# Another queue for the loads of a bias slab, another engine for three constant fills, in a one-core decoder layer

## The chip, the cores and the metric

The kernel runs on one core of a Trainium2 chip. The metric is the device time of one execution in microseconds (us); the time of the kernel before is the median of 3 runs. A profile of one execution comes with it; its times count from the start of its span. Engines go by the profile's names: PE (TensorE, matmuls), PEld (its weight loads), DVE (VectorE), ACT (ScalarE), POOL (GpSimd), SP (SyncE). ACTq, SPq and POOLq are DMA issues that stand in the instruction list of ACT, SP or POOL.

## The reference, cut to what matters

One layer on a batch of 1, 256 tokens, width 2048, in float32. Three sub-layers follow each other; each ends in a layer norm:

```python
mix = hybrid_mixer(h, ...)                       # S5 | stick-breaking | NSA, one projection in, one out
h = layer_norm(ALPHA * h + mix, ...)
h = layer_norm(ALPHA * h + memory_cross_attention(h, mem, ...), ...)
h = layer_norm(ALPHA * h + conv_ffn(h, ...), ...)
```

In the mixer the columns of one input projection go to an S5 state-space group (a scan over time, a GELU and a gate `z * sigmoid(z @ w_glu + b)`), to 8 stick-breaking attention heads, and to 16 NSA heads. Each NSA head has three branches (compressed, selected and window keys), and the same relative-position bias, looked up by the distance `t - s`, is added to the logits of all three:

```python
s_s = jnp.einsum('bqgrd,bgqmd->bgrqm', qb, ks) * scale + bias_s
p_s = masked_softmax(s_s, dist_s >= 0)
```

## The kernel before, in words

**Matmuls.** Every weight matrix is streamed from HBM in chunks of 128 x 1024 floats (512 KB) by `weights` (L266): SP loads a chunk into one of 4 buffers `raw`, ACT rounds it into one of 3 buffers `hi` (L291), DVE subtracts to get the rest, `lo` (L292, 3 buffers), and PE multiplies three times for each pair of tiles, hi with hi, hi with lo, lo with hi (`mm3`, L306 to L308: 24 matmuls for a chunk). The result stands in one of 3 PSUM tiles `pj`.

**Order of the work.** A scheduler puts the instructions of each engine in a fixed list before the run, by priority lanes and by a timeline of its own; on the chip each engine works through its list in that order and waits in place for what an instruction needs.

**The stretch in question** lies in `mixer` (L509) and runs from about 200 to 385 us. `s5_out` (L755) computes two NSA key projections (`nsa_keys`, L941: ACT casts them into `kh` at L938, DVE makes the rest `kl` at L939), closes the S5 scan (its last output is `s5u`), takes its GELU on ACT (L765) after which a table of functions is loaded (L253), and multiplies by `w_glu`: four tiles `pj`, each of 12 matmuls, each evicted by ACT (L782) and worked on by DVE (an addition L784, two reciprocals L786, a product L787). Then `nsa_queries` (L964) projects the 16 heads' queries (8 pairs of chunks) into `nq` (ACT L970, DVE L971), and `nsa` (L974) runs the attention: for each head a pair of matmuls for each of two query tiles into a PSUM tile `mx` (L1011, L1012; 2 buffers), then DVE adds the bias from `slab` and takes row minima (L1015, L1017), copies the compressed scores into `tcs` (L1023), ACT takes exponentials, and so on. Projection matmuls that need no attention result stand between those of the attention.

**The bias slab.** `nsa_bias` (L839) computes the bias of each head by distance and writes 16 shifted copies of it to DRAM (`g_dr`). `nsa_slab` (L951) loads `slab`, 128 rows x 16 heads x 256 floats (2 MB), in 8 loads, each of 16 rows x 16 heads x 1 KB, so that row p holds the bias shifted by p. The tile takes the memory of `Es` (L639), the sines of the S5 part, which PE reads last in the S5 output matmuls (L685, in the trace L190). All three `V.memset` of the change stand at the head of `nsa`: `pc` (128 x 1024 floats, zero; written later by L1087, read by PE at L1059) and the first halves of two tiles `tcs` (128 x 60 floats).

Of the kernel before, what the change touches and what calls it, by code (L numbers as in the profile page):

```python
# [25 lines left out]
BIG = 1e30  # L26
# [138 lines left out]
class Parts:  # L165
# [9 lines left out]
    def range(self, k, n):  # L175
        if k == 0 and self.first is not None:
            assert n == 1
            return self.first
        return self.tiles[k // self.n][:, k % self.n:k % self.n + n]
# [18 lines left out]
class Program:  # L198
# [310 lines left out]
    def mixer(self):  # L509
# [6 lines left out]
        with ExitStack() as nsa:  # L516
            self.nsq = pool(nsa, "nsq", 1)
            self.slabp = pool(nsa, "slabp", 1)
            with ExitStack() as s5:
                self.s5p = pool(s5, "s5p", 1, "right")  # L520
                self.s5w = pool(s5, "s5w", 2, "right")
                self.s5_tables()
                self.load_x()
                with ExitStack() as st:
                    self.sbp = pool(st, "sbp", 1)
                    self.sbw = pool(st, "sbw", 2)
                    self.stick_breaking()
                self.nsk = pool(nsa, "nsk", 1)
                self.nsa_compress()
                self.nsa_values()  # L530
                self.s5_out()
            self.resp = pool(self.ctx, "resp", 1, "right")
            self.R = self.resp.tile([128, 2, D], F32, name="R")
            self.mixq = pool(self.ctx, "mixq", 1, "right")
            self.mix += [self.mixq.tile([128, 4, 2, 256], F32R, name=f"mix{i}")
                         for i in range(2, 4)]
            with ExitStack() as st:
                self.nsp = pool(st, "nsp", 1, "right")
                self.nsw = pool(st, "nsw", 2, "right")
                self.nsa_slab()  # L540
                self.nsa_queries()
                self.nsa()
# [408 lines left out]
    def nsa_slab(self):  # L951


        g_dr, n = self.g_dr, 128 // SKEW

        self.nq = self.nsp.tile([128, 8, 2, 256], F32R, name="nq")
        self.slab = self.slabp.tile([128, NH, 256], F32, name="slab", tag="Es")
        with self.lane("first"):
            for c in range(n):
                src = bass.AP(g_dr.tensor, g_dr.offset + 127 - c,  # L960
                              [[384 - n, SKEW], [SKEW * 384, NH], [1, 256]])
                self.nc.scalar.dma_start(self.slab[c:128:n], src)

    def nsa_queries(self):  # L964
        a, V, S, q = self.a, self.nc.vector, self.nc.scalar, self.nq
# [8 lines left out]
    def nsa(self):  # L974
        nc, a, V, S = self.nc, self.a, self.nc.vector, self.nc.scalar
# [8 lines left out]
        def qcol(h):  # L984
            return 4 * (h // 8) + 2 * (h // 4 % 2) + h % 2


        pc = p.tile([128, 2, NH, 32], F32, name="pc")
        V.memset(pc, 0.0)
        tcs = [p.tile([128, 2, 4, NC_], F32, name=f"tcs{i}") for i in range(2)]  # L990
        for t in tcs:
            V.memset(t[:, 0], BIG)
        halves = lambda t: t.rearrange("p (c k) -> p c k", c=2)
        for quad in range(4):
            o = self.pq.tile([128, 2, 256], F32, name="pa")
            start = [None, None]
            for b in range(2):
                n = 128 if b else 128 + NK
                for gl in range(2):
# [3 lines left out]
                    for r in range(2):  # L1003
                        h = h0 + r
                        kh, kl = (k[:, h // 8, gl].rearrange("p c n -> p (c n)") for k in ks[b])
                        t = qcol(h)
# [329 lines left out]
```

## Time and profile before

| | |
|---|---|
| median of 3 runs | 1294.0 us (1293.86 to 1295.22) |
| the profiled execution's own time | 1293.79 us |
| its span in the trace | 1292.0 us |
| mean granted TensorE clock | 0.992 of full speed |
| busy, share of the span | PE 97%, PEld 90%, DVE 68%, ACT 51%, POOL 1% |
| moved by DMA | 237.37 MB, mean 184 GB/s |

The own time is what the runs are timed by; the span is what the trace shows of it, and 1.8 us lie around it. Busy shares are means over stages with different limits. A group of instructions with the same line and form is shown with its count; "idle before <-X" names what ended the idle time of the engine just before.

### The profile page before, as it was taken

Reading aid. Unit: us, or ns where it says so; the run is one execution under the profiler, and the core shown is the slowest. Engines: PE = TensorE matmul, PEld = TensorE weight load, DVE = VectorE, ACT = ScalarE, POOL = GpSimd, SP = SyncE. Lnnn points to the kernel's source line nnn. Section 1 sums busy time; section 2 is a strip of 40 time slices with the busy share of each in tenths; the row PEclk is TensorE's granted clock in tenths of the full one; section 3 lists DMA queues with packets and bytes.
Section 4 is the critical chain, followed back from the end, with each engine's and each line's share of the span. In section 5 each row is a group of like instructions: output and inputs, shape, how many; then the busy total and the mean of one; then the engine's idle time right before and its main releaser. Section 6 shows DMA issues by size and latency. Waiting matters only on the chain.

```text
span 1292.0 us, 23010 instructions
## 1 busy us (share of the span) xinstructions
PE 1254.6 (97%) x9222; PEld 1160.8 (90%) x9222; DVE 883.8 (68%) x1510; ACT 659.9 (51%) x1032; POOL 13.3 (1%) x23
## 2 busy tenths in 40 slices
PE   7999999999999999899999999999999999999996
PEld 7788898988779899799999999999999988888896
DVE  7799896877765675776666666666666654544557
ACT  6884434666554355455555555555555543334342
POOL 0200000000000000000000000000000000000000
PEclk9999999999999999999999999999999999999998
DMA  8653348633447564445555565565655755656573
GB/s 306 192 167 128 99 137 224 186 117 103 131 168 279 189 208 151 137 142 194 192 192 195 196 195 191 191 193 194 196 196 190 254 193 195 195 184 199 187 228 130
DMA packets 68886, 237.37 MB, mean 184 GB/s; under 512 B 7787, under 2 KB 10652, under 8 KB 68012
## 3 DMA queue, kind: packets, MB, share of 16 engines
q1 hardware_dynamic: 64720, 230.21, 53.7%
q10 hardware_dynamic: 3276, 3.47, 1.2%
q0 software_dynamic: 784, 2.23, 0.9%
q8 instruction: 72, 1.18, 0.4%
q14 instruction: 34, 0.28, 0.1%
HBM read 231.82 MB, written 2.49 MB: 181 GB/s over the span
## 4 chain that ended last, share of the span: by engine, by line
PE 76%; DVE 3%; ACT 1%; issue 1%; DMA 0%; DVEq 0%; ACTq 0%
PE pj L306 14%; PE pj L307 14%; PE pj L308 14%; PE pj L314 9%; PE pj L316 9%; PE pj L315 9%; PE pa L1048 2%; DVE lo L292 1%; PE mx L1011 1%; PE mx L1012 1%; DVE R L1144 1%; DVE R L1149 1%; PE op L1041 0%; PE pb L1041 0%; ACT hi L291 0%
## 5 line engine op out<-in xcount | busy, mean ns | idle before, releaser
L292 DVE TENSOR_TENSOR lo<-raw,hi 128x1024 fp32r<-128x1024 f32 (+2 forms) x403 | 488.5, 1212 | 339.0 <-ACT hi L291 337.9
L291 ACT CAST hi<-raw 128x1024 fp32r<-128x1024 f32 (+2 forms) x403 | 419.8, 1042 | 510.7 <-PE pj L307 276.4
L307 PE MATMUL pj<-mix,hi 128*128 128x256 f32 x1380 | 381.9, 277 | 0.0
L306 PE MATMUL pj<-mix,hi 128*128 128x256 f32 x1380 | 381.1, 277 | 0.0
L308 PE MATMUL pj<-mix,lo 128*128 128x256 f32 x1380 | 381.0, 276 | 0.0
L307 PEld LDWEIGHTS pj<-mix,hi 128*128 128x128 f32 x1380 | 259.2, 188 | 0.1
L308 PEld LDWEIGHTS pj<-mix,lo 128*128 128x128 f32 x1380 | 259.2, 188 | 0.1
L306 PEld LDWEIGHTS pj<-mix,hi 128*128 128x128 f32 x1380 | 259.1, 188 | 0.2
L306 PE MATMUL pj<-A,hi 128*128 128x256 f32 x496 | 141.2, 288 | 8.6 <-ACT hi L291 8.6
L308 PE MATMUL pj<-A,lo 128*128 128x256 f32 x496 | 139.2, 288 | 4.2 <-DVE lo L292 4.0
L307 PE MATMUL pj<-A,hi 128*128 128x256 f32 x496 | 140.4, 286 | 0.0
L306 PEld LDWEIGHTS pj<-A,hi 128*128 128x128 f32 x496 | 95.9, 194 | 11.2 <-ACT hi L291 9.3
L308 PEld LDWEIGHTS pj<-A,lo 128*128 128x128 f32 x496 | 94.6, 194 | 8.1 <-DVE lo L292 5.6
L307 PEld LDWEIGHTS pj<-A,hi 128*128 128x128 f32 x496 | 96.1, 194 | 1.9 <-issue 1.9
L315 PE MATMUL pj<-lo,act 128*128 128x512 f32 (+1 forms) x280 | 96.8, 347 | 0.0
L316 PE MATMUL pj<-hi,act 128*128 128x512 f32 (+1 forms) x280 | 96.8, 347 | 0.0
L315 PE MATMUL pj<-lo,A 128*128 128x512 f32 (+2 forms) x288 | 96.3, 336 | 0.0
L316 PE MATMUL pj<-hi,A 128*128 128x512 f32 (+2 forms) x288 | 95.6, 333 | 0.0
L314 PE MATMUL pj<-hi,A 128*128 128x512 f32 (+2 forms) x288 | 91.0, 334 | 0.0
L314 PE MATMUL pj<-hi,act 128*128 128x512 f32 (+1 forms) x280 | 89.7, 347 | 0.0
L315 PEld LDWEIGHTS pj<-lo,A 128*128 128x128 f32 x288 | 54.1, 188 | 6.5 <-issue 1.1
L315 PEld LDWEIGHTS pj<-lo,act 128*128 128x128 f32 x280 | 52.9, 189 | 6.6
(324 smaller groups left out, 1809.5 us busy)
## 6 DMA issues: line engine op xcount, KB each, us to landing
raw<-in_w_up SPq DMA_DIRECT2D x176, 512.0 KB, 4.2
raw<-in_w_down SPq DMA_DIRECT2D x92, 512.0 KB, 3.3
raw<-in_win_c SPq DMA_DIRECT2D x48, 512.0 KB, 3.9
raw<-in_w_out SPq DMA_DIRECT2D x32, 512.0 KB, 4.0
raw<-in_win_sv SPq DMA_DIRECT2D x8, 512.0 KB, 4.7
raw<-in_wk_m SPq DMA_DIRECT2D x8, 512.0 KB, 4.9
raw<-in_wv_m SPq DMA_DIRECT2D x8, 512.0 KB, 4.2
raw<-in_wq SPq DMA_DIRECT2D x8, 512.0 KB, 4.1
```

Of the source, the lines that this page charges most:

```text
L291: self.last_hi = nc.scalar.copy(hi[:, :n], raw[:, :n])
L292: self.last_lo = nc.vector.tensor_sub(lo[:, :n], raw[:, :n], hi[:, :n].bitcast(F32))
L306: mm(ps, hi, ah, start=start, stop=False)
L307: mm(ps, hi, al, start=False, stop=False)
L308: self.last_mm = mm(ps, lo, ah, start=False, stop=stop)
L314: mm(ps, ah, hi, start=start, stop=False)
L315: mm(ps, ah, lo, start=False, stop=False)
L316: self.last_mm = mm(ps, al, hi, start=False, stop=stop)
L1011: mm(zs, q[:, t, gl, qs], kh[:, 0:m], start=True, stop=False)
L1012: mm(zs, q[:, t, gl, qs], kl[:, 0:m], start=False, stop=True)
L1048: ins = mm(o[64 * r:64 * r + 64, gl, 128 * c:256], vv[:, c, v, :], pt[:, k0:k1], start=start[r] is None, stop=False, skip_group_check=True)
L1144: ins = V.scalar_tensor_tensor(r, r, mean, self.gb[:, 0, c0:c1], ALU.subtract, ALU.mult)
```

## The change

The 8 loads of `slab` are issued by POOL and no longer by ACT, and the three constant fills at the head of `nsa` run on POOL and no longer on DVE. Sizes, addresses and results are the same.

```diff
@@ nsa_slab
             for c in range(n):
                 src = bass.AP(g_dr.tensor, g_dr.offset + 127 - c,
                               [[384 - n, SKEW], [SKEW * 384, NH], [1, 256]])
-                self.nc.scalar.dma_start(self.slab[c:128:n], src)
+                self.nc.gpsimd.dma_start(self.slab[c:128:n], src)
@@ nsa
         pc = p.tile([128, 2, NH, 32], F32, name="pc")
-        V.memset(pc, 0.0)
+        nc.gpsimd.memset(pc, 0.0)
         tcs = [p.tile([128, 2, 4, NC_], F32, name=f"tcs{i}") for i in range(2)]
         for t in tcs:
-            V.memset(t[:, 0], BIG)
+            nc.gpsimd.memset(t[:, 0], BIG)
```

The scheduler then writes other lists for PE, DVE and ACT from here to the end of the mixer. SP's list is the same, and PE's is the same up to the second attention head. Three places follow, rows of the lists as they stand, without the number at their start; tiles that share a buffer pool are told apart by numbers.

ACT's list where S5 ends, one piece of the difference (- before, + changed). `kh_2091` is the first key tile, `s5u<-s5u` the GELU:

```order
 L938 CAST kh_2091<-pj 64x2x128 x2
-L962 DMA slab<-g_dr 16x16x256 x8
-L291 CAST hi<-raw 128x1024 x2
-L938 CAST kh_2091<-pj 64x2x128 x2
 L765 ACTIVATE s5u<-s5u 128x1024
 L253 ACT_TABLE_LOAD
 L979 ACTIVATE gate<-gate 128x96
 L291 CAST hi<-raw 128x1024
```

The eight loads leave ACT's list, and the GELU with its table load now stands ahead of the two weight casts and the key casts that were behind the loads. On POOL the eight loads stand right behind its last instruction so far, the memset of `kl_2544`, and behind them the fills of `pc` and of the two `tcs`, which are the last work of POOL in the program.

DVE's list at the gate of the S5 part, before and changed. `s5z_2705` and `s5z_2726` are the gate tiles of the first two `w_glu` results, and `kl1_2544<-pj_2613` frees the PSUM tile that the first query projection, `pj_2803`, takes:

```order
L784 TENSOR_SCALAR s5z_2705<-s5z_2705 128x256
L786 RECIPROCAL s5z_2705<-s5z_2705 128x128 x2
L939 TENSOR_TENSOR kl1_2544<-pj_2613,kh1_2543 64x256
L292 TENSOR_TENSOR lo_2837<-raw_2834,hi_2836 128x1024
L787 TENSOR_TENSOR s5z_2705<-s5z_2705,s5u_198 128x256
L784 TENSOR_SCALAR s5z_2726<-s5z_2726 128x256
```

```order
L784 TENSOR_SCALAR s5z_2705<-s5z_2705 128x256
L786 RECIPROCAL s5z_2705<-s5z_2705 128x128 x2
L292 TENSOR_TENSOR lo_2837<-raw_2834,hi_2836 128x1024
L784 TENSOR_SCALAR s5z_2726<-s5z_2726 128x256
L939 TENSOR_TENSOR kl1_2544<-pj_2613,kh1_2543 64x256
L787 TENSOR_TENSOR s5z_2705<-s5z_2705,s5u_198 128x256
```

The subtraction that frees the PSUM tile now stands behind a weight chunk's `lo` and behind the addition of the second gate tile.

PE's list at the first attention heads, before and changed. `mx_3348` is the tile of the second head and `mx_3385` that of the third; `pj_2998` is the fourth query projection:

```order
L1011 MATMUL mx_3348<-kh0_2091,nq_2793 128x272
L1012 MATMUL mx_3348<-kl0_2092,nq_2793 128x272
L1011 MATMUL mx_3385<-kh0_2091,nq_2793 128x256
L1012 MATMUL mx_3385<-kl0_2092,nq_2793 128x256
L1011 MATMUL mx_3385<-kh0_2091,nq_2793 128x272
```

```order
L1011 MATMUL mx_3348<-kh0_2091,nq_2793 128x272
L1012 MATMUL mx_3348<-kl0_2092,nq_2793 128x272
L306 MATMUL pj_2998<-A_92,hi_3001 128x256
L307 MATMUL pj_2998<-A_92,hi_3001 128x256
L308 MATMUL pj_2998<-A_92,lo_3002 128x256
```

Before, the third head follows the second at once; now a whole chunk, 24 projection matmuls, stands between them. From here to the end of the attention its matmuls are spread over more projection matmuls than before.

## Rows read from the trace of the kernel before

**Rows 1.** The page's busy time of each engine, with its share of the span and its instructions.

```profile
PE 1254.6 (97%) x9222; PEld 1160.8 (90%) x9222; DVE 883.8 (68%) x1510; ACT 659.9 (51%) x1032; POOL 13.3 (1%) x23
```

**Rows 2.** Busy time by stretch: the stretch, its length, busy us (and instructions begun) of PE, PEld, DVE, ACT and POOL, then the granted PE clock, the share of the 16 DMA engines and GB/s.

```profile
222.00:224.00 2.00, 0.45 (x4) 0.24 (x3) 0.00 (x0) 0.41 (x1) 0.00 (x0) 1.00 1.09 201
224.00:226.00 2.00, 0.56 (x3) 0.35 (x3) 1.33 (x2) 1.96 (x4) 0.00 (x0) 1.00 1.15 197
226.00:228.00 2.00, 2.00 (x10) 2.00 (x11) 1.45 (x2) 1.96 (x3) 0.00 (x0) 0.53 1.15 193
228.00:230.00 2.00, 2.00 (x13) 2.00 (x13) 0.90 (x3) 1.99 (x4) 0.00 (x0) 0.62 1.08 217
232.00:234.00 2.00, 1.49 (x14) 1.32 (x13) 1.93 (x3) 1.40 (x3) 0.00 (x0) 1.00 0.91 305
234.00:236.00 2.00, 1.23 (x11) 1.01 (x9) 1.49 (x2) 1.84 (x4) 0.00 (x0) 1.00 0.45 113
236.00:238.00 2.00, 0.76 (x6) 0.77 (x7) 1.90 (x5) 1.79 (x5) 0.00 (x0) 1.00 0.77 254
258.00:260.00 2.00, 1.50 (x13) 1.28 (x11) 1.97 (x8) 1.46 (x3) 0.00 (x0) 1.00 0.51 186
260.00:262.00 2.00, 0.00 (x0) 0.00 (x0) 1.97 (x9) 1.95 (x8) 0.00 (x0) 1.00 0.69 256
262.00:264.00 2.00, 1.52 (x11) 1.55 (x12) 1.84 (x8) 1.02 (x5) 0.00 (x0) 0.91 0.77 215
264.00:266.00 2.00, 2.00 (x12) 2.00 (x11) 1.96 (x10) 0.99 (x4) 0.00 (x0) 0.50 0.13 53
266.00:268.00 2.00, 2.00 (x15) 2.00 (x15) 0.43 (x4) 0.04 (x1) 0.00 (x0) 0.73 0.00 0
270.00:384.00 114.00, 114.00 (x742) 91.98 (x742) 81.41 (x302) 70.82 (x192) 0.00 (x0) 1.00 0.38 125
```

**Rows 3.** Who waited for whom, PE alone, from 195 to 260 us and then from 260 to 420 us: us in total, times, longest.

```profile
PE pj L306 <- ACT hi L291: 2.2, 1, 2.2
PE pj L306 <- ACT s5z L782: 2.0, 1, 2.0
PE pj L308 <- DVE lo L292: 0.8, 1, 0.8
PE pj L306 <- DVE kl L939: 0.5, 1, 0.5
...
PE mx L1011 <- DVE nq L971: 3.0, 1, 3.0
```

**Rows 4.** ACT's instructions in order of time: start, length, instruction, and the idle time before it.

```profile
214.40 9.10 ACTq L962 DMA_DIRECT2D slab<-g_dr  x8
223.59 1.99 ACT L291 CAST hi<-raw 128x1024 fp32r<-128x1024 f32 x2 [9.04 <-DMA slab<-g_dr]
226.38 1.06 ACT L765 ACTIVATE s5u<-s5u 128x1024 f32<-128x1024 f32 x1
227.45 1.28 ACT L253 ACT_TABLE_LOAD   x1
236.71 0.47 ACT L782 ACTIVATE s5z<-pj,s5nbg 128x256 f32<-128x256 f32 x1
250.29 1.06 ACT L291 CAST hi<-raw 128x1024 fp32r<-128x1024 f32 x1 [1.29 <-PE pj L307]
253.01 1.06 ACT L291 CAST hi<-raw 128x1024 fp32r<-128x1024 f32 x1 [1.25 <-PE pj L307]
```

**Rows 5.** The instructions that write or read `slab`: count, ns least/median/most, first and last start, forms; and the time from issue to landing of its loads.

```profile
L1015 DVE CUSTOM_DVE_ANT_0 tt<-mx,slab x32: 259/285/292, 259.3 to 361.1; 128x128 f32<-128x128 f32 x32
...
L962 ACTq DMA_DIRECT2D slab<-g_dr x8: 540/630/1221, 214.4 to 223.0; - x8
...
DMA to landing us min/median/max: 8.5/10.3/12.2
```

**Rows 6.** DVE's instructions in order of time, columns as in rows 4.

```profile
214.96 0.47 DVE L190 SCALAR_TENSOR_TENSOR s5u<-s5u,s5prm,pa 128x256 f32<-128x256 f32 x1
...
224.67 2.36 DVE L292 TENSOR_TENSOR lo<-raw,hi 128x1024 fp32r<-128x1024 f32 x2 [8.78 <-ACT hi L291]
...
237.24 0.28 DVE L784 TENSOR_SCALAR s5z<-s5z 128x256 f32<-128x256 f32 x1
237.55 1.76 DVE L786 RECIPROCAL s5z<-s5z 128x128 f32<-128x128 f32 x2
239.34 0.43 DVE L939 TENSOR_TENSOR kl<-pj,kh 64x256 fp32r<-64x256 f32 x1
...
256.03 0.91 DVE L989 MEMSET pc<- 128x1024 f32 x1 [0.16 <-DVE lo L292]
```

**Rows 7.** The loads that POOL issues early in the program, of the S5 inputs (128 KB each): count, ns least/median/most, first and last start; and from issue to landing.

```profile
L496 POOL DMA_DIRECT2D s5us<-Ec x12: 550/551/693, 35.4 to 42.5; - x12
...
DMA to landing us min/median/max: 3.3/5.3/8.8
```

**Rows 8.** Busy time by stretch, columns as in rows 2, for the gate of the S5 part and for the time of POOL's early loads.

```profile
235.00:258.00 23.00, 20.86 (x179) 20.45 (x179) 21.27 (x35) 13.37 (x24) 0.00 (x0) 1.00 0.52 170
34.00:44.00 10.00, 10.00 (x49) 8.33 (x48) 6.34 (x10) 8.73 (x17) 6.69 (x12) 1.00 0.88 224
```

**Rows 9.** POOL's last instruction, a fill of 128 x 1024 floats.

```profile
181.93 0.95 POOL L931 MEMSET kl<- 128x1024 f32 x1 [15.32 <-PE mx L877]
```

## The prediction

> **What bounds the kernel now.** I read the busy shares first [rows 1]. PE is busy 97% of the span, the other engines far less, so a change counts only where PE stands still or runs slowly near it. I therefore read the busy time by stretch around the loads of `slab` [rows 2]. From 270 to 384 us PE is busy 114.00 of 114 us at clock 1.00: work taken off DVE or ACT there buys nothing. The losses lie ahead of that, in 222 to 268 us. Next I asked who waited for whom [rows 3], and then read the waiting engines in order of time. ACT spends 9.10 us, from 214.40 on, on issuing the eight loads, and its next weight cast comes at 223.59 after 9.04 us [rows 4]. DVE, whose `lo` needs that cast, does nothing for 8.78 us up to 224.67 [rows 6]. PE uses up the chunks cast ahead and then stands.
>
> **PE's losses, as they are.** Each is the length of a stretch less its busy time, or the busy time times what the clock lacks to 1.00 [rows 2].
> 1. PE out of weights, 222 to 226 us: 1.55 + 1.44 = 3.0 us. By the waits, 2.2 for `hi` and 0.8 for `lo` [rows 3].
> 2. Just behind it the granted clock is 0.53 and 0.62, near the 1.2 GHz level, from 226 to 230: 0.94 + 0.76 = 1.7 us.
> 3. 232 to 238 us: 0.51 + 0.77 + 1.24 = 2.5 us; these are the waits for the key remainder (L939, 0.5) and for the eviction of the first gate tile (L782, 2.0).
> 4. 258 to 264 us: 0.50 + 2.00 + 0.48 = 3.0 us, the wait of an attention matmul for `nq` from L971. DVE is busy 1.97 us of each 2 there: it is still working off what the 8.78 us put back.
> 5. After that stop the clock is 0.50 and 0.73 from 264 to 268: 1.0 + 0.5, and 0.1 before it, is 1.6 us.
>
> Together 11.8 us.
>
> **The loads leave ACT.** `s5u` is written by 214.96 + 0.47 = 215.4 us [rows 6]. The GELU (1.06) and the table load (1.28) follow, then a small activation on 128 x 96, at most the 0.47 that the larger 128 x 256 takes, and the next weight cast, 1.06 [rows 4]. That cast ends by about 219.3, and its `lo`, 2.36/2 = 1.18 [rows 6], by about 220.5. PE ran dry only at about 222.4 [rows 2]. So losses 1 and 2 go whole; the cover is some 2 us.
>
> **The gate stretch.** The changed list of DVE puts `kl1_2544<-pj_2613` behind a `lo` and a second L784. The wait of loss 3 thereby moves: the second and third gate tiles need PSUM tiles long free, and the tile waited for is the one that the first query projection takes. DVE does, behind the eviction of the first gate tile (0.47 on ACT [rows 4]), 0.28 + 1.76 (L784 and the reciprocals) + 1.18 (`lo`) + 0.28 + 0.43 (L939) [rows 6]: 3.93 us, with the eviction 4.4, and with hand-over between engines, which I estimate at 0.1 to 0.6 in all, 4.5 to 5.0. Meanwhile PE has three gate tiles of 12 matmuls. A chunk's 24 matmuls set the 2.72 us from one cast to the next, 250.29 to 253.01 [rows 4], so 36 take 4.08. The new wait is 0.4 to 0.9; I take 0.9. The eviction of the second gate tile can stand behind a weight cast of 1.06 on ACT: between 0 and 1.06, I take 0.4, since PE has one more tile to work on. For the third head, 24 matmuls (2.72 us) now come ahead of the matmul that waited 3.0: I keep 0.2. New losses: 1.5 us, between 0 and 4.7, the upper end being one whole stop such as 4 with its slow clock, 3.0 + 1.7.
>
> **The loads on POOL.** POOL's last work is a fill at 181.93 [rows 9], so it waits for the same end of the S5 matmuls that ACT waited for and begins at about 214.3. Its earlier loads took 0.55 us each to issue [rows 7]: eight are 4.4 us on an engine with nothing queued but the fills. No row shows loads of this shape on POOL, so I bound their landing. Below: 214.3 + 4.4 + 5.3 (the median landing) = 224. Above: the twelve early loads, 1.5 MB in all, take from 35.4 to 42.5 + 8.8 = 51.3, which is 15.9 us [rows 7], scaled to 2 MB 21.2 us, so 235.5. I take 235, as those are the nearest rows. The first reader is L1015, at 259.3 before [rows 5]; with losses 1 to 3 gone (7.2) and the new 1.3 added it stands at about 253.4. That leaves 18 us of cover. If it were gone, each us late would be a us of PE.
>
> The same bytes share the DMA engines with the weight stream: 2 MB over some 18 us are 117 GB/s, and a chunk of 0.524 MB every 2.72 us is 193. The sum, 310, stands against 305 in the best stretch of two us [rows 2]. The chunks that lie ready in 3 `hi` and 4 `raw` buffers cover up to 19 us, so I put this at nothing; its price is in rival A.
>
> **The fills.** DVE loses a fill of 0.91 [rows 6] and two small ones. POOL does the large one in 0.95 [rows 9], at a time when it is otherwise idle, and the tiles are read only in the attention. DVE's gain lies in loss 4 and isn't counted again.
>
> **Sum.** 11.8 - 1.5 = 10.3 us. The profiled execution's own time is 1293.8, 0.2 below the median: 1293.8 - 10.3 = 1283.5 us.
>
> **Rivals.**
> A. *One stop stays.* Either DVE still is late with `nq`, or the weights come late while `slab` loads. For it: DVE is busy 21.27 of 23 us from 235 to 258 [rows 8], so it works off a debt slowly, and 310 GB/s is at the edge. Against: DVE starts 8.8 us earlier. One stop with its slow clock costs 4.7, the gain is 5.6 to 5.8 and the time 1288.
>
> B. *Hardly any gain.* The idle time is only displaced: the attention, whose lists are rewritten, gives it back. From 270 to 384 PE has no idle time that could hide an added wait, DVE is busy 81.41 and ACT 70.82 of 114 [rows 2], so there is room, which speaks against it. A gain of 10.3 less two stops of 4.7 would be 0.9: 1292.9.
> The Trainium skill, in "DMA: Bandwidth & Descriptors", section "Issuing engines are not separate DMA queues", says that issuing on several engines saves only the issuing sequencer's time, which is usually small beside the transfer. By that the change would bring almost nothing, about 1293 us. This trace differs on the size: 9.10 us on ACT against 8.5 to 12.2 from issue to landing [rows 4, 5].
>
> C. *Slower.* POOL could issue only while DVE stands still. From 235 to 258 DVE leaves 1.73 us of 23 [rows 8], a share of 0.075, so 4.4 us of issuing would need 58 us: the last load is issued at about 273, lands 8.8 later at 281.6, and L1015, due at 253.4, waits 28.2, with 1.7 for the clock behind it. Less the 10.3 gained that is 19.6 slower: 1313. It decides from a landing at about 262 on, 48 us after the start and over twice my upper bound. Against it: POOL's early issues kept to 550 to 693 ns while DVE was busy 6.34 of 10 us [rows 7, 8].
> The Trainium skill names such a mechanism in "SBUF — State Buffer", section "SBUF: two separate sides": a load issued from GpSimd has its descriptors written there, and this stops while VectorE runs an operation in a mode that takes both ports. By it the time would lie between 1283 and 1313, depending on how many of DVE's operations are of that kind, which no row here shows.
>
> **How the numbers follow.** The forecast as worked out has 0.62, A 0.23, B 0.06, C 0.04, and a gain above 12 us, which would need something outside the sum, 0.05. The forecast's own bounds are 1282.0 (no new loss) to 1285.2 (new losses of 3.2, between the 1.5 taken and the 4.7). For 8 in 10 the range reaches down to 1281.0, a little of the larger gain, and up over A to 1288.5; out of it fall B, C and the rest of the larger gain. A measurement of this kernel tells about 0.2% from no change, 2.6 us. Faster by more: the forecast, A and the larger gain, 0.90. Within: B and a part of C, 0.06. Slower: 0.04, the rest of C and mishaps of its size.
>
> **What would show it.** ACT has no 9 us gap at 214, and the GELU starts at about 215.4. PE is busy 2.00 of 2 us from 222 to 230 at clock 1.00. PE's largest wait in the gate is that of the first query projection for L939, below 1 us, and the wait of L1011 for L971 shrinks from 3.0 to a few tenths. L1015 first runs at about 253. POOL's eight issues take about 0.55 us each and the last load lands by 235. If PE's busy time grows by as much as its idle time falls, or the stretch after 264 has a slow clock again, the sum is wrong, and A or B holds; if L1015 waits for `slab`, C.

## The result, and the profile after

The changed kernel takes 1286.15 us (median of 4 runs, 1285.80 to 1287.67), the kernel before 1293.93 on the same chip: the ratio is 0.994, with a 95% interval from 0.9923 to 0.9957. The gain is 7.8 us. Forecast were 10.3 and 1283.5; the time lies in the range, between the forecast and rival A.

The page's first line, as [rows 1]:

```profile
PE 1251.7 (98%) x9222; PEld 1158.2 (90%) x9222; DVE 882.1 (69%) x1507; ACT 660.3 (51%) x1032; POOL 18.9 (1%) x34
```

Busy time by stretch in the changed kernel, columns as in [rows 2]:

```profile
222.00:224.00 2.00, 2.00 (x20) 2.00 (x19) 1.94 (x3) 1.95 (x5) 0.00 (x0) 1.00 1.00 201
224.00:226.00 2.00, 2.00 (x20) 2.00 (x19) 1.24 (x2) 0.17 (x1) 0.00 (x0) 1.00 1.07 213
226.00:228.00 2.00, 2.00 (x20) 2.00 (x19) 0.86 (x1) 1.79 (x3) 0.00 (x0) 1.00 1.04 240
228.00:230.00 2.00, 2.00 (x19) 2.00 (x18) 0.80 (x2) 0.00 (x0) 0.00 (x0) 1.00 1.00 252
230.00:232.00 2.00, 0.79 (x7) 0.58 (x5) 0.00 (x0) 0.59 (x1) 0.00 (x0) 1.00 1.05 283
232.00:234.00 2.00, 0.23 (x2) 0.23 (x2) 1.48 (x2) 1.66 (x4) 0.00 (x0) 1.00 1.04 293
234.00:236.00 2.00, 1.47 (x12) 1.26 (x11) 1.97 (x4) 0.85 (x1) 0.00 (x0) 1.00 0.96 313
236.00:238.00 2.00, 1.38 (x11) 1.38 (x12) 1.91 (x4) 1.30 (x4) 0.00 (x0) 1.00 0.42 162
...
260.00:262.00 2.00, 2.00 (x20) 2.00 (x19) 1.97 (x8) 0.99 (x4) 0.00 (x0) 1.00 0.26 102
...
264.00:266.00 2.00, 2.00 (x15) 1.49 (x15) 1.87 (x5) 2.00 (x8) 0.00 (x0) 1.00 0.23 92
```

From 222 to 230 us PE is now busy throughout at clock 1.00, and so it is from 258 to 270. What is left lies between 230 and 238 us: PE stands 1.21 + 1.77 + 0.53 + 0.62 = 4.1 us, in two pieces of 2.98 and 1.15 us, with no slow clock behind them. I call the two together the stop in the gate. The losses of 11.8 us have become 4.1, which is 7.7 us; the span fell by 8.4 (1292.0 to 1283.6) and the median by 7.8.

Who waited for whom in that stretch (answers to [rows 3]; us in total, times, longest):

```profile
ACT hi L291 <- DMA raw<-in_win_c: 5.0, 2, 3.5
...
PE pj L306 <- ACT s5z L782: 4.1, 2, 3.0
...
ACT hi L291 <- DMA raw<-in_w_glu: 1.9, 1, 1.9
```

ACT in order of time (answers to [rows 4]):

```profile
215.28 1.06 ACT L765 ACTIVATE s5u<-s5u 128x1024 f32<-128x1024 f32 x1 [0.91 <-DVE s5u L190]
216.35 1.28 ACT L253 ACT_TABLE_LOAD   x1
...
217.84 1.03 ACT L291 CAST hi<-raw 128x1024 fp32r<-128x1024 f32 x1
...
231.41 1.04 ACT L291 CAST hi<-raw 128x1024 fp32r<-128x1024 f32 x1 [3.53 <-DMA raw<-in_win_c]
...
233.25 0.47 ACT L782 ACTIVATE s5z<-pj,s5nbg 128x256 f32<-128x256 f32 x1
```

The waits name the eviction L782 as what PE stood for. The order in time shows what is behind it. PE had finished the tile by 230.8. Its eviction stands in ACT's list behind a weight cast, and that cast waited 3.53 us for its chunk to arrive. The second piece comes about in the same way: the next L782 stands behind the next cast, which waited 1.43 us for its chunk. The stop is a late weight load, seen through ACT's fixed list.

Where the chunk was: the DMA queues in three stretches of 2 us of the changed kernel, from 216, 224 and 232 us (q1 carries SP's weight loads, q0 POOL's `slab`; packets, MB, share of the 16 engines; below them the loads issued in the stretch, with the us from issue to landing):

```profile
q1 hardware_dynamic: 75, 0.29, 42.0%
q0 software_dynamic: 51, 0.17, 35.8%
slab<-g_dr POOLq DMA_DIRECT2D x5, 256.0 KB, 14.8
...
q0 software_dynamic: 128, 0.41, 103.5%
q1 hardware_dynamic: 2, 0.00, 1.2%
raw<-in_win_c SPq DMA_DIRECT2D x1, 512.0 KB, 12.5
...
q1 hardware_dynamic: 147, 0.54, 94.5%
q0 software_dynamic: 14, 0.05, 9.2%
raw<-in_win_c SPq DMA_DIRECT2D x1, 512.0 KB, 6.2
```

The eight loads are all issued within 4.49 us. From 220 to 226 they have the DMA engines nearly to themselves, though weight loads issued at 220.16 and 223.14 stand ready. The one of 220.16 lands 11.2 us after issue and one of 224.85 12.5, against 4.4 for a chunk issued at 210. SP's issues around it (start, length):

```profile
214.88 0.33 SPq L772 DMA_DIRECT2D raw<-in_w_glu  x1
...
220.16 0.33 SPq L270 DMA_DIRECT2D raw<-in_win_c  x1
...
223.14 0.33 SPq L270 DMA_DIRECT2D raw<-in_win_c  x1
```

Of POOL itself (answers to [rows 7, 9]):

```profile
214.47 4.49 POOL L962 DMA_DIRECT2D slab<-g_dr  x8 [31.77 <-DMA raw<-in_win_c]
250.97 0.96 POOL L989 MEMSET pc<- 128x1024 f32 x1 [32.02 <-DVE s5z L787]
```

### The profile page after: what moved, and what is told of

Same layout as the page of the kernel before. It is cut to its first block, busy times and chain, and to the rows that moved or that the text cites. A ratio compares the mean times of both kernels' runs of the same rounds, so it can differ in the third digit from the quotient of the medians.

```text
span 1283.6 us, 23034 instructions
## 1 busy us (share of the span) xinstructions
PE 1251.7 (98%) x9222; PEld 1158.2 (90%) x9222; DVE 882.1 (69%) x1507; ACT 660.3 (51%) x1032; POOL 18.9 (1%) x34
## 4 chain that ended last, share of the span: by engine, by line
PE 92%; DVE 3%; ACT 2%; DMA 2%; issue 1%; SPq 0%; ACTq 0%; DVEq 0%
PE pj L306 17%; PE pj L308 17%; PE pj L307 17%; PE pj L314 10%; PE pj L315 10%; PE pj L316 10%; PE pa L1048 2%; DMA raw<-in_win_c 1%; PE pa L190 1%; PE mx L877 1%; ACT hi L291 1%; PE mx L1011 1%; DVE lo L292 1%; PE mx L1012 1%; DVE R L1144 0%
## 5 line engine op out<-in xcount | busy, mean ns | idle before, releaser
L306 PEld LDWEIGHTS pj<-A,hi 128*128 128x128 f32 x496 | 94.5, 191 | 8.2 <-ACT hi L291 6.3
L307 PEld LDWEIGHTS pj<-A,hi 128*128 128x128 f32 x496 | 94.5, 191 | 1.6 <-issue 1.6
L316 PEld LDWEIGHTS pj<-hi,act 128*128 128x128 f32 x280 | 52.9, 189 | 6.6
```

The lines of the kernel that those rows point to most:

```text
L306: mm(ps, hi, ah, start=start, stop=False)
L307: mm(ps, hi, al, start=False, stop=False)
L316: self.last_mm = mm(ps, al, hi, start=False, stop=stop)
```

## The experiments

Two theories stood against each other. Traffic: the weights are late because 2 MB are queued ahead of them at once. Order: the stop comes from the new lists, with evictions behind casts on ACT and a longer chain on DVE. In e3_no_loads, e4_twice, f_sp, g_sp and e5_sp_at_once the lists of PE, DVE and ACT agree with the changed kernel's row for row; g_sp is f_sp once more and g_changed the changed kernel once more. The changed kernel's two ratios, 0.9940 and 0.9958, are 2.3 us apart, with intervals that overlap; so a difference of that size from the changed kernel is not shown unless the two ran side by side. Ratios are to the kernel before on the same chip. The rows from e3_no_loads to e1_loads_only share a chip, so do those from e5_sp_at_once to e2_fills_only and those from h1_order to f_act. The last column is PE's busy time in the 20 us from 230 to 250 and the granted clock.

| kernel | issuer of `slab` | median, us | ratio (95%) | PE busy, clock 230 to 250 |
|---|---|---|---|---|
| changed | POOL at once | 1286.15 | 0.9940 (0.9923 to 0.9957) | 15.87, 1.00 |
| e3_no_loads | none | 1283.28 | 0.9917 (0.9897 to 0.9937) | 19.41, 1.00 |
| e4_twice | POOL, twice | 1290.50 | 0.9968 (0.9956 to 0.9980) | 15.49, 1.00 |
| f_sp | SP, spread | 1284.20 | 0.9927 (0.9905 to 0.9949) | 19.41, 1.00 |
| e1_loads_only | POOL at once | 1287.86 | 0.9954 (0.9941 to 0.9968) | 17.45, 0.91 |
| e5_sp_at_once | SP at once | 1289.15 | 0.9966 (0.9953 to 0.9979) | 15.41, 0.83 |
| g_sp | SP, spread | 1283.67 | 0.9926 (0.9912 to 0.9940) | 19.41, 1.00 |
| g_changed | POOL at once | 1288.21 | 0.9958 (0.9943 to 0.9972) | 16.21, 0.83 |
| e2_fills_only | ACT at once | 1289.76 | 0.9973 (0.9961 to 0.9985) | 17.84, 0.99 |
| h1_order | ACT at once | 1294.04 | 1.0006 (0.9990 to 1.0021) | 18.01, 1.00 |
| f_sp_dve | SP, spread | 1285.46 | 0.9940 (0.9917 to 0.9962) | 19.41, 1.00 |
| f_act | ACT, spread | 1286.29 | 0.9945 (0.9928 to 0.9962) | 19.10, 1.00 |
| i_before | ACT at once | 1293.94 | 0.9995 (0.9983 to 1.0006) | 18.23, 1.00 |

**e3_no_loads: take the traffic away.**

```diff
-            for c in range(n):
-                src = bass.AP(g_dr.tensor, ...)
-                self.nc.gpsimd.dma_start(self.slab[c:128:n], src)
+            self.nc.gpsimd.memset(self.slab, 0.0)
```

> Left out: the eight loads of slab; POOL fills slab with zeros instead (128 x 4096 floats, some 4 us on POOL). The lists of PE, DVE, ACT and SP are those of the changed kernel. Traffic theory: the stop of 4.1 us that PE has in the gate of the S5 part in the changed kernel (waits for L782 at 230.8 and 236) is there because the weight chunks come late behind the 2 MB of slab; without them ACT's weight casts wait under 1 us for raw, the stop shrinks to between 0 and 1.5 us, and the time is 1282.0 to 1283.7 us. Order theory: the stop comes from the new order (evictions behind weight casts in ACT's list, the longer chain on DVE); it stays at about 4 us and the time at 1286 us.

Measured: 1283.28 us, for a kernel that leaves the bias out and adds zeros in its place. Busy time from 230 to 240 us in e3_no_loads:

```profile
230.00:240.00 10.00, 9.41 (x79) 9.03 (x78) 9.56 (x15) 6.21 (x12) 0.00 (x0) 1.00 0.50 161
```

and the largest wait of PE that it shows in the gate:

```profile
PE pj L306 <- DVE kl L939: 0.6, 1, 0.6
```

With the same lists and no traffic the stop falls from 4.1 to 0.6 us, and what remains is the wait that the prediction named, for L939. The order theory is out for this stop.

**e4_twice: double it.**

```diff
-            for c in range(n):
+            for c in (*range(n), *range(n)):
```

> Each of the eight loads of slab is issued twice by POOL, 4 MB in place of 2; the lists of PE, DVE, ACT and SP are those of the changed kernel. Traffic theory: the weights get next to nothing for as long again (the slab's queue holds the DMA engines from about 219 to 237 instead of 228), weight chunks issued from 220 on land some 8 to 10 us later than in the changed kernel, PE's stop in the gate grows by 6 to 10 us with a slow clock of up to 1.7 us behind it, and the time is 1292 to 1298 us. Order theory: the stop stays as it is, 1286 us, as the doubled loads are still done long before the first L1015 at 255.

Measured: 1290.5 us, below the 1292 to 1298 expected. By the ratios that is 3.6 us above the first measurement of the changed kernel and 1.3 above the second, whose interval overlaps it widely; the changed kernel was not run on this chip, so the size is open. Waits of ACT and PE from 205 to 270 us:

```profile
ACT hi L291 <- DMA raw<-in_win_c: 14.6, 6, 4.7
...
PE pj L306 <- ACT s5z L782: 4.4, 2, 3.1
...
PE pj L306 <- DVE nq L971: 0.9, 1, 0.9
```

ACT waits twice as long for weights (14.6 us against 5.0 + 1.9), PE only a little longer (4.4 + 0.9 and 0.2 for a `lo`, 5.5 us in all against 4.1). The doubling was not a doubling of the queue: the second load of a row group waits until the first has landed, so POOL issued the second eight one by one, up to 236.4 us. From 228 to 230 us, with the loads coming singly, both got through at about the same rate, 0.26 MB of `slab` and 0.27 of weights. The expectation missed that; the next kernel uses it.

**f_sp: the same bytes, spread.** SP issues each load behind one weight load of the query projections; the fills stay on POOL.

```diff
+            if self.pending:
+                self.after(nc.sync.dma_start(*self.pending.pop(0)), self.last_load)
...
-                self.nc.gpsimd.dma_start(self.slab[c:128:n], src)
+                self.pending.append((self.slab[c:128:n], src))
```

> The eight loads of slab are issued by SP, one behind each of the first eight weight loads of the query projections (L272); the lists of PE, DVE and ACT are those of the changed kernel, the fills stay on POOL. Traffic theory: the same 2 MB, spread over some 20 us, let the weights through: ACT's casts wait under 1.5 us in all for raw, PE's stop in the gate falls from 4.1 to between 0 and 1.5 us, the time is 1282.0 to 1283.7 us; the last slab load lands at 240 to 250, ahead of the first L1015 at about 252. Order theory: 1286 us with the same stop. If the loads come too late instead, L1015 waits for slab, and the time is above 1284 us with that wait in the trace.

Measured: 1284.2 us, half a us above the expected stretch. The stop is 0.6 us, the wait for L939, as in e3_no_loads. Busy time of f_sp, and then the instructions that write or read `slab` with the time from issue to landing:

```profile
230.00:240.00 10.00, 9.41 (x79) 9.03 (x78) 9.56 (x15) 6.21 (x12) 0.00 (x0) 1.00 1.07 237
```

```profile
L1015 DVE CUSTOM_DVE_ANT_0 tt<-mx,slab x32: 257/281/294, 252.6 to 359.2; 128x128 f32<-128x128 f32 x32
L272 SPq DMA_DIRECT2D slab<-g_dr x8: 543/544/654, 221.6 to 241.2; - x8
...
DMA to landing us min/median/max: 6.1/8.5/9.3
```

The DMA engines are as full as before (share 1.07), yet no cast waits for a chunk here. In g_sp, the same kernel, casts do wait for chunks:

```profile
ACT hi L291 <- DMA raw<-in_win_c: 4.0, 3, 2.2
```

PE's stop in the gate is 0.6 us there too, so those waits are covered. The last load is issued at 241.2 and lands by 250.5 at the latest, two us ahead of its first reader at 252.6.

**e5_sp_at_once: f_sp's queue, but all eight loads in a row.**

```diff
-                self.nc.gpsimd.dma_start(self.slab[c:128:n], src)
+                self.after(self.nc.sync.dma_start(self.slab[c:128:n], src), self.last_load)
```

> SP issues all eight loads of slab in a row, behind the second load of w_glu and ahead of the first weight chunk of the query projections; lists of PE, DVE and ACT as in the changed kernel. It has the time of issue of the changed kernel and the queue of f_sp. Traffic theory (what counts is that 2 MB are queued ahead of the weights at once): weight chunks issued behind them land 8 to 12 us after issue, PE stops for 3 to 6 us in the gate, and the time is within 1.5 us of the changed kernel or above it. Queue theory (loads from POOL's queue push the weights aside, loads from SP's queue do not): the stop is under 1.5 us as in f_sp, some 2 to 3 us faster than the changed kernel.

> f_sp once more beside the changed kernel on one chip: by the traffic theory 2 to 3.5 us faster than it, PE's stop in the gate 0.6 us.

> The changed kernel once more, as the measure for g_sp and e5_sp_at_once on the same chip: 0.6% (0.4 to 0.8) below the kernel before, the stop of about 4 us in the gate as before.

Measured side by side: 1289.15, 1283.67 and 1288.21 us. PE's waits for L782, in e5_sp_at_once and then in g_changed:

```profile
PE pj L306 <- ACT s5z L782: 4.6, 1, 4.6
```

```profile
PE pj L306 <- ACT s5z L782: 3.8, 2, 3.1
```

In both the granted clock is 0.83 over the 20 us from 230 on, a mean of the two levels 1.2 and 2.4 GHz, after PE had stood; in the first profile of the changed kernel it stayed at 1.00 after a stop of the same length. Behind the stop of g_changed:

```profile
238.00:240.00 2.00, 2.00 (x11) 2.00 (x11) 1.94 (x5) 0.01 (x1) 0.00 (x0) 0.50 0.45 115
240.00:250.00 10.00, 10.00 (x79) 10.00 (x77) 7.58 (x13) 4.96 (x8) 0.00 (x0) 0.85 0.41 141
```

That is 1.0 + 1.5 us lost to the slow clock, with 0.6 in the two us before it 3.1. Queued all at once, the loads stop PE from either queue; the 0.9 us between the two times lie within their intervals. The two are not alike in all else: SP is busy issuing the eight up to 222.8, and its next weight load comes 7.6 us behind the one before, where it is 5.3 in the changed kernel; a part of e5_sp_at_once's stop may come from that. g_sp is 4.5 us below the changed kernel here, with intervals that do not meet, and a us more than expected: it is spared this slow clock too. One rival stays open: the spread loads of f_sp also start some 6 us later than POOL's, counted from the second load of `w_glu`, and no run queues all eight at once that late.

**e1_loads_only and e2_fills_only: one edit each.** The diff of each is one half of the change's.

> Only the loads go to POOL; the three fills stay on DVE. The prediction counted the fills at nothing: 1286.2 us, within 0.7 of the changed kernel, with the same stop of about 4 us in the gate. If the fills matter (DVE is busy nearly all of 235 to 258 us), the first attention matmuls wait for DVE and it is 1 us or more above the changed kernel.

> Only the three fills go to POOL; ACT still issues the loads. The prediction counted the fills at nothing. ACT is held 9 us and PE loses its weights at 222 to 226 as in the kernel before; 0 to 1.1 us below the kernel before (the fill of 0.91 us and two small ones stood on a busy DVE ahead of the wait for nq at 260). If the fills were part of the gain, 2 us or more below.

Measured: 1287.86 us for the loads alone. By the ratios that is 1.8 us above the first measurement of the changed kernel, where up to 0.7 was expected, and 0.5 below the second; all three intervals overlap, so no difference is shown. Its stop in the gate is 2.5 us. For the fills alone 1289.76 us: 3.5 us below the kernel before, where 0 to 1.1 were expected. Busy time from 222 and from 250 us in e2_fills_only:

```profile
222.00:230.00 8.00, 5.14 (x31) 4.73 (x30) 2.78 (x3) 5.08 (x7) 0.00 (x0) 0.80 1.14 198
...
250.00:270.00 20.00, 20.00 (x173) 19.58 (x171) 19.39 (x56) 14.08 (x35) 1.12 (x3) 1.00 0.51 175
```

Losses 1 and 2 are as before. Loss 4, the stop for `nq`, is gone. In e1_loads_only its wait is 0.2 us. So either edit removes it. The two parts (about 6 and 3.5 us) add up to more than the whole (7.8, and 5.4 by g_changed), which fits that both take out the same stop.

**h1_order: is loss 4 a matter of order or of 1.1 us of fills?** The kernel before, and one rule for the scheduler.

```diff
+ h or b or self.after(first, self.rest)      # first: first L1015; rest: L971 of the second query projection
```

(Cut to the rule; two more lines give `first` and `rest` their names.)

> The kernel before with one more rule for the scheduler and nothing else: DVE's first L1015 stands behind the L971 of the second query projection (L971, L1015). ACT issues the loads and DVE does the fills as before; DVE's list changes from its 355th row on and PE's from the second head on, with a chunk of projection matmuls ahead of the third head, as in the fills-only kernel. Order theory: the stop at 258 to 264 us and the slow clock behind it (4.6 us) depend on the order of these lists; both go, and the time is 3 to 5 us below the kernel before, as in the fills-only kernel. Work theory: they depend on the 1.1 us that the fills cost DVE just ahead; the wait for L971 stays at 2 us or more and the gain is under 1.5 us.

Measured: no change, 1.0006. The stop of 3.0 us became one of 1.9, a projection's wait in place of the third head's:

```profile
PE pj L306 <- DVE nq L971: 1.9, 1, 1.9
```

Neither theory's numbers hold whole; the work theory comes nearer (2 us or more of wait, under 1.5 us of gain). The rule put a second `lo` (1.2 us) ahead of L971, and the fills (1.1 us) still stand ahead of both, so the matmul chunk that now covers the wait is not enough. In e2_fills_only neither stands there. That both count is how I read the two lists; no run here takes only the second `lo` away, and the split stays open.

**f_sp_dve and f_act: the fills without a stop near, and ACT as the issuer with spread loads.**

```diff
-        nc.gpsimd.memset(pc, 0.0)
+        V.memset(pc, 0.0)
...
-                self.after(nc.sync.dma_start(*self.pending.pop(0)), self.last_load)
+                self.after(nc.scalar.dma_start(*self.pending.pop(0)), self.last_load)
```

(f_sp_dve has the first of these and the two small fills likewise, f_act the second.)

> As f_sp (SP issues the loads, one behind each weight chunk), with the three fills left on DVE. The fills by themselves, with no stop near them: DVE works 1.1 us more at about 252 us, where the first head waits for it; between 0 and 1.1 us above f_sp, which was 9.7 us below the kernel before. If the fills on POOL are worth more than that, 2 us or more above f_sp.

> ACT issues the loads as in the kernel before, but one behind each of the first eight weight loads of the query projections instead of all in a row; fills on POOL. Traffic theory: what cost the kernel before were eight issues in a row behind each other (9.1 us); spread, each holds ACT for 0.5 to 1.2 us and the weights pass, so PE's stop in the gate is under 2 us and the time within 1.5 us of f_sp. If issuing on ACT costs wherever it stands, evictions and casts are late by a us or more each time, PE stops for 3 us or more, and the time is 1286 us or above.

Measured: 1285.46 us for f_sp_dve, by the ratios 1.7 above f_sp with intervals that overlap, a little over the 1.1 expected; its trace has no stop that f_sp and g_sp lack (0.8 us of standing PE from 200 to 300 us, against 0.6 and 0.9). And 1286.29 for f_act, 2.3 us above f_sp where the traffic theory allowed 1.5; here too the intervals overlap. Its stop in the gate is 0.9 us, as that theory has it, but its other lists bring back the stop for `nq` (waits of f_act, then its loads of `slab`):

```profile
PE mx L1011 <- DVE nq L971: 2.7, 1, 2.7
...
PE pj L306 <- ACT s5z L782: 0.9, 1, 0.9
```

```profile
L272 ACTq DMA_DIRECT2D slab<-g_dr x8: 539/540/632, 220.1 to 239.3; - x8
```

So the time of 1286 us or above, which was to show that issuing on ACT costs wherever it stands, came about in another way. Spread over 19 us, an issue holds ACT for 0.54 us; all in a row the same eight took 9.10 us [rows 4].

**i_before: how far apart two executions of one kernel lie.**

> The kernel before itself once more, as a control: how far apart two executions of the same instructions lie. Expected: ratio 1.000 within 0.2%; the same 8.6 us of standing PE from 214 to 270 us, with slow clocks of 1.7 and 1.6 us behind the two stops. Open is the slow clock at 540 to 560 us, in the memory attention, which is 0.91 in the first trace and 0.83 to 0.84 in the traces of most other kernels here: if it is 0.83 here too, it belongs to the execution, and what the order kernel lost there was not its own; if it is 0.91, the earlier kernels gave some 1.5 us back there.

Measured: 0.9995. The stops come again, with 7.7 us of standing PE where 8.6 were expected (the wait for L782 is 1.2 us, in the first trace 2.0). The clock behind them does not always fall again:

```profile
258.00:264.00 6.00, 3.03 (x26) 2.84 (x25) 5.78 (x24) 4.88 (x16) 0.00 (x0) 1.00 0.56 190
264.00:270.00 6.00, 6.00 (x53) 5.87 (x53) 5.75 (x28) 4.39 (x15) 0.00 (x0) 1.00 0.15 31
...
540.00:560.00 20.00, 16.59 (x104) 14.59 (x104) 15.14 (x31) 10.93 (x24) 0.00 (x0) 0.83 0.19 61
```

After the same 3.0 us of standing the clock from 264 on is 1.00 here and was 0.50 and 0.73 in [rows 2]; at 540 to 560 us it is 0.83 here and was 0.91 in the first trace. So the 0.83 that h1_order and others show there need not come from an edit: two executions of one kernel differ by as much. One profile against another can differ by 1.6 us at such a place.

## Why the prediction was right, and where it was not

**The loads leave ACT: right.** The GELU starts at 215.28 us (forecast 215.4), the next cast ends at 218.87 (by 219.3 at the latest), and losses 1 and 2 are gone whole, 4.7 us.

**The gate: the wait named is there, another was missed.** The wait for L939 was put at 0.4 to 0.9 us and is 0.6 in e3_no_loads and f_sp, where nothing hides it. The 0.4 for the second gate tile does not appear there. e3_no_loads, which has the changed kernel's lists and lacks the loads, is 10.7 us below the kernel before by its ratio (8.2 to 13.3 by the interval), where 10.3 were forecast: without the traffic the forecast holds.

**The traffic beside the weights: the step that failed.** The prediction put it "at nothing", because "the chunks that lie ready in 3 `hi` and 4 `raw` buffers cover up to 19 us". Its price is 4.1 - 0.6 = 3.5 us of standing; where a slow clock follows, as in g_changed, that comes on top. Two things were wrong in it. It took the buffers for a full cushion, though a chunk can be asked for only when a `raw` buffer comes free. From 214.88 to 220.16 SP asked for none, and what it asked for then stood behind `slab`. And it compared means, 310 GB/s against 305, as if the loads and the weights were served side by side. What decides here is what is queued ahead of what: f_sp moves the same 2 MB beside the weights and PE does not stop for them, though its DMA engines are the fuller. Over 205 to 260 us, first the changed kernel and then f_sp, where SP's queue carries both:

```profile
q1 hardware_dynamic: 2676, 9.77, 56.5%
q0 software_dynamic: 640, 2.10, 18.6%
...
q1 hardware_dynamic: 4987, 12.30, 81.4%
```

The first two lines also give a price. That is 0.565 x 55 / 9.77 = 3.2 us of all 16 engines for a MB of weights, and 4.9 us for a MB of `slab`. An estimate from these for the 23 us from the first issue to the last landing (214.5 to 237): 8.5 chunks of 0.524 MB take 14.2 and `slab` 10.2, together 24.4 us in 23. So there was no room to spare. But there is none in f_sp either, and it has no such stop.

So the mechanism is the second half of rival A ("the weights come late while `slab` loads"). Its price had a whole stop with its slow clock, 4.7 us; the first profile shows the stop without the clock, g_changed with it. The Trainium skill says in "DMA: Bandwidth & Descriptors", section "Issuing engines are not separate DMA queues", that loads end up on the same 16 DMA engines whichever engine starts them. The runs agree: 4.1 and 3.8 us of standing from POOL's queue, 4.6 from SP's. The same section of the Trainium skill calls the issuing time, which is all that issuing from several engines saves, usually small beside the transfer. In this case it was not small: 9.10 us on ACT, against 8.5 to 12.2 from issue to landing [rows 4, 5].

**The loads on POOL: right.** Issues take 0.56 us each (forecast 0.55). The loads land 7.8 to 18.8 us after issue, the last by about 237 (taken: 235), far ahead of L1015 at 255.3. Rival C did not come: POOL's issues were as short as in [rows 7] while DVE was busy 5.47 of the 8 us from 214 on.

**Losses 4 and 5: gone, as forecast.** But loss 5, the clock behind the stop, was no fixed property of the kernel before, as i_before shows; 1.6 of the 11.8 us belong to that one execution.

**The fills: put too low.** "Isn't counted again" was right for the sum. That an edit of 1.1 us could bring 3.5 us by itself, by taking DVE off the path ahead of a stop and by other lists, was not seen.

The sum with the measured terms: 11.8 - 4.1 = 7.7 us, against the 7.8 of the medians. The wrong term was 2.6 us of 10.3, the difference of 4.1 and 1.5. That the sum meets the medians to 0.1 us is in part luck: the first profile of the kernel before had a slow clock behind loss 4, and the first of the changed kernel had none behind its stop. The second profiles give 7.7 + 1.6 = 9.3 us (i_before) and 3.8 + 3.1 = 6.9 (g_changed), a gain of 2.4 us in this stretch, where the ratio beside g_changed says 5.4. And the time lies in the range because the range was drawn up over rival A, not because the sum had the stop.

## What to carry to other kernels

A block of loads that is moved off a busy engine can stall the same consumer again as traffic: price it in time on the DMA engines, from a row with packets and share, and ask which loads will be queued behind it. Where its reader is far off, issue it piece by piece between the loads that are urgent: here that, with a start 6 us later, was worth 3.5 us of PE standing, at equal bytes and equal lists of PE, DVE and ACT. And when the waits name an evicting engine, read its list back in time: what it stood behind was a load.

The version that does so (f_sp, and again as g_sp: loads from SP between the weight chunks, fills on POOL) has the lowest ratio of those here that load `slab`, 0.74% below the kernel before (g_sp 0.9926, 0.9912 to 0.9940); the intervals of f_sp_dve, of f_act and of the first measurement of the changed kernel overlap with it.

## What the runs showed of the hardware beyond this

- A block queued at once from one queue held up the loads of another: from 222 to 226 us of the changed kernel the weight loads on SP's queue got 0.02 MB and less in 2 us, while POOL's queue moved 0.37 and 0.41. It is not simply that what is issued first is served first: the second load of `w_glu`, issued at 214.88, ahead of seven of the eight loads, took 11.1 us to land there and 3.9 in f_sp. In e4_twice both queues moved about the same from 228 us on. What decides between these two cases is not shown.
- The same `slab` is 640 packets when POOL issues it and 2176 when ACT does, and takes 18.6% and 21.3% of 55 us on the DMA engines when issued at once; from ACT spread out (f_act) it takes 16.0%, so these shares are not a price of the packets alone.
- After stops of the same length the granted clock fell in one execution (0.50 and 0.73 from 264 us) and stayed at 1.00 in another of the same kernel.
